# Transposes of 32x32 blocks on VectorE in the block inverse of a delta-rule decoder step

## Chip, cores and metric

The kernel runs on one core of a Trainium2 chip. The metric is the device time of one execution in microseconds; times before are the median of 3 runs. The engines are named as in the profile: PE is TensorE's matmuls, PEld its weight loads, DVE is VectorE, ACT is ScalarE, POOL is GpSimd, SP is the engine whose queue issues most DMAs.

## What is computed

One inference step of a hybrid decoder with two layers, 256 prompt tokens and 8 sequences of 8 sample tokens, all fp32. Each layer projects the tokens once (2048 to some 7000 columns), runs three groups of heads on the columns, projects back, adds, normalizes and runs a SwiGLU block. The change lies in the first group, the gated delta rule (6 heads of 128). Its core, for chunks of C tokens:

```python
gcum = jnp.cumsum(gi, axis=1)
dmat = jnp.exp(jnp.where(tri, gh[..., :, None] - gh[..., None, :], -jnp.inf))
kk = jnp.einsum('bihd,bjhd->bhij', ki, ki)
A = jnp.where(strict, kk * dmat * bh[..., :, None], 0.0)
M = jnp.eye(C, dtype=jnp.float32) + A
...
sol = lax.linalg.triangular_solve(M, jnp.concatenate([vbeta, kbd], -1),
                                  left_side=True, lower=True, unit_diagonal=True)
```

The kernel builds the inverse T of M, a lower triangular matrix with a unit diagonal, from the inverses of its 32x32 diagonal blocks.

## The kernel before

**Dense work.** The 320 tokens are the moving columns of all projections. Every weight is split into a high and a low part in a format that PE multiplies at its fast rate: ScalarE copies the high part (`whi`), VectorE subtracts to get the low part (`wlo`), and each 128x128 weight block gives three matmuls of 128x320, named `xh,whi`, `xl,whi` and `xh,wlo` in the profile. Weights arrive as units of four blocks (128x512, buffer `raw`), twelve matmuls each. There are four buffers of low parts, and the splits run three units ahead of the matmuls.

**Mixers.** The three groups of heads are generators that issue small operations while the dense matmuls of the input and output projection run. Everything is first recorded. A planner (`Program.order`) then puts all operations in an order by its own cost estimates and by the longest tail behind each operation, and only this order is issued; every engine works through its own rows strictly in that order. For PE the planner prefers dense matmuls while small ones of less than the full array collect, and then issues the collected ones together. This document calls one such run of small matmuls between two dense ones a visit. The small matmuls are fp32, and the profile counts each of them as two instructions. Line 671 issues all planned operations, so the profile gives that line to almost everything; the names of the tiles tell operations apart.

**The inverse.** `gdn_prompt` calls `inverse` for two chunks of 128 tokens in each of two half groups of three heads, `gdn_sample` once for each half with 64 tokens; with two layers that makes 8 calls of 128 rows (R) and 4 of 64 rows, each for 3 heads (k). The result `TU` holds T in `tu[:, 0]` and its transpose in `tu[:, 1]`, both as 32x32 blocks side by side: partitions are the rows of the blocks, columns are 3 heads x 32. The algorithm starts with blocks of size 1 and doubles the size. `lt[:, s]` is the part of A (transposed) that level s couples. The start sets T to I - L, for which the transpose of `lt[:, 0]` is made on PE as a matmul with the identity (`cs("idb")`); T's transpose is made by POOL without PE. Each later level (4 with 128 rows, 2 with 64 rows) has two halves on PE: first `lt[:, s]` times T, which ScalarE copies out of PSUM into `p_`; then T times `p_`, and in further matmuls the transpose of that product (`pw[:, 0]` and `pw[:, 1]`). One VectorE subtraction of both parts (192 columns) updates T and its transpose. A half level is one 32x32x32 matmul for each block and head, 12 in the prompt, 6 with the sample tokens.

The users of `TU` multiply with both parts. After both groups of prompt and sample, `gate` multiplies the outputs with the gate and splits them into `oA`, which the output projection reads first.

**Names in the profile.** `g` (in orders `g_0_90`) is the memory of `gdn_prompt`; `c` (`c_0_92`), `blkC` and `gen` hold that of `gdn_sample`; `cst` holds constants, the identity blocks among them; `geng` holds attention and linear-attention data; `bank` is PSUM.

Of the kernel before, what the change touches and what calls it, by code (L numbers as in the profile page):

```python
# [23 lines left out]
D = 2048  # L24
# [96 lines left out]
class Mem:  # L121
    """columns of one SBUF tile handed out and taken back in program order, longest-free or (fit) smallest first"""
# [4 lines left out]
    def alloc_top(self, n):  # L127
        """from the highest end"""
        for a, m, t in sorted(self.free, reverse=True):
            if m >= n:  # L130
                self.free.remove((a, m, t))
                if m > n:
                    self.free.append((a, m - n, t))
                return (a + m - n, n, self.ap[:, a + m - n:a + m])
        return None
# [45 lines left out]
class Clock:  # L181
    """rough engine times, used only to choose the order in which work is issued"""
# [56 lines left out]
class TagTile:  # L239
    """a tile of a tag, made when its turn comes in the final order"""  # L240
# [5 lines left out]
class LazyAP:  # L246
    """access pattern of a TagTile: a stand-in for shapes, and the steps that lead to the real one"""
# [53 lines left out]
def region(ap):  # L301
    """(memory, first and last partition, [(first column, last column)]) of an access pattern"""
    key = None
    if isinstance(ap, LazyAP):
        key, ap = ap.h.key, ap.ap_
    if not isinstance(ap, bass.AP):
        ap = ap[:]
    if "DRAM" in str(ap.space):
        return None
    dims = [tuple(d) for d in ap.ap]  # L310
    w, npart = dims[0]
    p0, c0 = divmod(ap.offset, w)
    run, outer = 1, []
    for s, n in sorted(dims[1:]):
        if n == 1 or s == 0:
            continue
        if s == run or s < run:
            run = (n - 1) * s + run
        else:
            outer.append((s, n))  # L320
    starts = [c0]
    for s, n in reversed(outer):
        starts = [x + s * i for x in starts for i in range(n)]
    if key is not None:
        c = 0
    return (key or ap.name, p0, p0 + npart, [(x, x + run) for x in starts])
# [14 lines left out]
class Program:  # L341
    """operations as they are asked for, put in another order that keeps what they depend on, then issued"""
# [6 lines left out]
    # ---- dependencies  # L349
# [19 lines left out]
    def epoch(self, key):  # L369
        """a bank begins a new use"""  # L370
        if self.seen.get(key):
            self.pre[key] = self.seen[key]
        self.seen[key] = []
        self.mem.pop(key, None)
        for q in range(4):
            self.chain.pop((key, q), None)
# [45 lines left out]
    def _merge(self, g, o, reads, writes, quads):  # L422
        """o runs beside g, in other columns of the array"""
        deps = set()
        for w, aps in ((False, reads), (True, writes)):
            for ap in aps:
                r = region(ap)
                key, p0, p1, spans = r
                if key.startswith("bank"):
                    spans = [(0, 512)]  # L430
                    deps.update(self.pre.get(key, ()))
                    self.seen.setdefault(key, []).append(g.i)
                if w:
                    for q in quads:
                        if (key, q) in self.chain:
                            deps.add(self.chain[(key, q)])
                        self.chain[(key, q)] = g.i
                self._touch(g.i, key, w, p0, p1, spans, deps, g.raw)
        deps.discard(g.i)
        g.preds |= deps  # L440
        g.subs.append((o.fn, o.a, o.kw))
        g.quads = sorted(set(g.quads) | quads)
        i = g.i
        self._cost(o, False, 1)
        g.cost = max(g.cost + 24, o.cost)
        g.busy += 24
        g.load = max(g.load, o.load)
# [62 lines left out]
    # ---- order  # L510
    def order(self):
# [42 lines left out]
        while len(res) < len(ops):  # L554
# [15 lines left out]
            # choose  # L570
# [103 lines left out]
def aps_of(name, a, kw):  # L674
    """(read, written) access patterns of an operation"""
# [43 lines left out]
def emit(nc, pool, psp, T, O, coff, ioff, n_pages):  # L719
# [53 lines left out]
    # ---------------------------------------------------------------- helpers  # L773
# [20 lines left out]
    def rsqrt_small(out, v):  # L794
        """out = v ** -0.5 for a few columns"""
        r0 = 64 if out.shape[0] == 64 else 0
        tt(G, out, v, cs("mhalf", slice(r0, 128)).to_broadcast([128 - r0, out.shape[1]]), ALU.pow)
# [4 lines left out]
    # ---------------------------------------------------------------- tasks  # L802
# [73 lines left out]
    def fb(*bs):  # L876
        for b in bs:
            mix_free.append(b)
# [9 lines left out]
    # ---------------------------------------------------------------- units  # L888
# [5 lines left out]
    def four(W, u, keys, ln):  # L894
        """four output blocks, all of them one k at a time; x is not normalized yet where ln is given"""
# [6 lines left out]
    def one(W, u, key, nk, x, pre=None):  # L902
        """one output block over nk k-blocks, four at a time"""
# [61 lines left out]
    # ---------------------------------------------------------------- weight stream  # L965
# [19 lines left out]
    # ---------------------------------------------------------------- evictions  # L985
# [62 lines left out]
    def small_block(i, key):  # L1048
        """32 outputs: the k-blocks side by side in the four column groups, which stay four partial sums"""
# [15 lines left out]
    # layer norm, first half: t = acc - c for a c near the mean of the token, and its sums. The product that  # L1065
    # follows starts on g t before the sums are known: W (g (t - mu) r + b) = r (W (g t) - mu W g) + W b, with
    # -g and b as two more columns of x
# [79 lines left out]
    def ln_scale(m, e):  # L1147
        """t -> (t - mu) r"""
# [61 lines left out]
    def block_value(key, bi):  # L1210
        """(values, per-row term still to be added or None, memory to free) of a finished block"""
# [72 lines left out]
    # ================================================================ mixers  # L1284
# [60 lines left out]
    # ---------------------------------------------------------------- GDN  # L1345
    # q, k, v are kept as 2 silu(.) = x (1 + tanh(x / 2)); the l2 norm of q and k takes the factor out
# [59 lines left out]
    def gdn_main(l):  # L1406
# [38 lines left out]
        # cumulative decays  # L1445
# [19 lines left out]
        # l2 norms (the blocks hold twice the vectors: 4 eps)  # L1465
# [25 lines left out]
        # output gate  # L1491
# [7 lines left out]
    def gate(l, hi, lo, z, o):  # L1499
        """out = hi/lo of o * z (1 + tanh(z / 2))"""  # L1500
# [18 lines left out]
    def inverse(aq, k, R, get, keep):  # L1519
        """aq: [R, k, 2, N] with A^T at [:, :, 1]; returns handle of TU [R, 2, k, 32] (T | T^T) of the 32-blocks"""  # L1520
# [18 lines left out]
        bb = yield from bank()  # L1539
        pv_ = banks[bb][0:R, 0:32 * k].rearrange("p (h i) -> p h i", h=k)  # L1540
        for h in range(k):
            for b in range(nb):
                sl = slice(32 * b, 32 * b + 32)
                mm(pv_[sl, h], lt[sl, 0, h], cs("idb", sl))
        tt(G, tu[:, 1], idb, lt[:, 0], ALU.subtract)
        tt(V, tu[:, 0], idb, pv_, ALU.subtract)
        fb(bb)
# [3 lines left out]
        for s in range(1, nl):  # L1551
# [10 lines left out]
            pw = banks[bb][0:R, 0:64 * k].rearrange("p (t h i) -> p t h i", t=2, h=k)  # L1562
            for h in range(k):
                for b in range(nb):
                    sl = slice(32 * b, 32 * b + 32)
                    mm(pw[sl, 0, h], tu[sl, 1, h], p_[sl, h])
                for b in range(nb):
                    sl = slice(32 * b, 32 * b + 32)
                    mm(pw[sl, 1, h], p_[sl, h], tu[sl, 1, h])
            tt(V, tu, tu, pw, ALU.subtract)  # L1570
            fb(bb)
            yield
# [3 lines left out]
    def decay_scores(l, g, h0, k, get, keep):  # L1576
        """[R, k, 2, n]: D * s_j * (q k^T | k k^T)^T of token group g, heads h0..h0+k"""
# [31 lines left out]
    def rms_factor(m, out, t1, c=None):  # L1609
        """out = c * rsqrt(c^2 m / 128 + 1e-6) (c = 1 where not given)"""  # L1610
# [10 lines left out]
    def gdn_prompt(l, hs):  # L1621
# [6 lines left out]
        for c in range(2):  # L1628
# [50 lines left out]
            # token-major keys (scaled for the state update) and values  # L1679
# [21 lines left out]
            # right-hand side  # L1701
# [67 lines left out]
    def gdn_sample(l, hs):  # L1769
# [10 lines left out]
        # the upper rows of these columns hold the outputs  # L1780
# [68 lines left out]
    # ---------------------------------------------------------------- differential attention  # L1849
    lam_init = [0.8 - 0.6 * math.exp(-0.3 * l) for l in range(DEPTH)]  # L1850

    def hilo(hi, lo, src, g=None):
        """hi/lo split of src (times the per-partition column g)"""
# [7 lines left out]
    def rope_pair(l, j, t):  # L1861
        """rotate blocks j and j + 1; t holds their rows in the partners' places (zeros where sin is zero)"""
# [12 lines left out]
    def attn_main(l):  # L1875
# [27 lines left out]
        # V of this step, token major  # L1903
# [117 lines left out]
    def attn_scores(l, lsel, getb, get1):  # L2021
# [13 lines left out]
        for pr in range(4):  # L2035
            # q of the two sequences, laid out so that other sequences and maps meet zeros
# [56 lines left out]
    def attn_values(l, vt, getb):  # L2093
# [3 lines left out]
        for quad in range(2):  # L2097
# [35 lines left out]
            # rows of the transpose are (b4, h, q); the output wants (h, b, q)  # L2133
# [9 lines left out]
    # ---------------------------------------------------------------- gated linear attention  # L2143
    def gla_main(l):
# [26 lines left out]
        # running log decay, feature major [128 (2 heads x 64), 3 blocks, tokens]  # L2171
# [28 lines left out]
    def gla_prompt(l, bc, eb, M1):  # L2200
# [10 lines left out]
        # score matrices, transposed: [j, head, i] for both chunks and for the sample tokens  # L2211
# [57 lines left out]
        # k e^{last - bc} (token major) and q e^{bc}  # L2269
# [155 lines left out]
    # ---------------------------------------------------------------- run  # L2425
# [177 lines left out]
```

## Time and profile before

| | us |
|---|---|
| runs: median (lowest, highest) | 3383.41 (3383.02, 3388.16) |
| profiled execution, span from first to last instruction | 3386.1 |
| busy: PE | 3292.8 (97%) |
| busy: DVE | 1976.8 (58%) |
| busy: ACT | 1484.9 (44%) |
| busy: POOL | 596.7 (18%) |
| granted TensorE clock, mean | 0.990 |

The span falls into stretches that repeat with the layer: input projection and mixers (0 to 600 and 1690 to 2270 us), output projection with the end of the mixers and a layer norm (to 780 and 2460 us), and the SwiGLU block (to 1690 and 3386 us). In the SwiGLU blocks PE is busy with dense matmuls alone. In the first two, dense matmuls and visits take turns. A busy share is a mean over these stretches; the cost of one visit is read from the timeline of PE, where rows are in order of start time and equal instructions in a row are merged ("x24").

### The profile page before, as it was taken

The numbers are of one execution on the slowest core, as the hardware profiler recorded it, in microseconds if no ns is written. First come the engines' busy times: TensorE is split into PE (matmuls) and PEld (weight loads), VectorE is DVE, ScalarE is ACT, GpSimd is POOL, SyncE is SP. The second block draws the span as 40 slices with busy tenths as digits, with TensorE's granted clock in tenths as the row PEclk, the third lists the DMA queues.
The fourth block names the chain that finished last, engine by engine and source line by source line (L and its number), as shares of the span: only waits on it lengthen the run. The fifth ranks groups of instructions, "written<-read, shape, count | busy, mean of one in ns | idle before, by whom it ended". The sixth has DMA issues, their size and how long they took to land. (4 is left out here: it accounts for less than half of the span.)

```text
span 3386.1 us, 70352 instructions
## 1 busy us (share of the span) xinstructions
PE 3292.8 (97%) x26570; PEld 3101.2 (92%) x26570; DVE 1976.8 (58%) x3624; ACT 1484.9 (44%) x3059; POOL 596.7 (18%) x825
## 2 busy tenths in 40 slices
PE   9999999999999999999999999999899999999996
PEld 8888787889999999999988887878899999999996
DVE  6666448786445444444876664587954454444446
ACT  5444444445433443344564443453644334433443
POOL 0233423260000000000523333231600000000005
PEclk9999999999999999999999999999999999999998
DMA  6455753434454554544444567434344545454443
GB/s 217 140 175 184 243 189 123 138 118 147 150 150 150 151 150 150 150 150 150 146 145 139 177 213 242 155 116 153 118 147 150 150 150 152 151 150 150 150 150 109
DMA packets 264696, 527.89 MB, mean 156 GB/s; under 512 B 31394, under 2 KB 33570, under 8 KB 264226
## 3 DMA queue, kind: packets, MB, share of 16 engines
q1 hardware_dynamic: 243874, 456.26, 43.8%
q0 software_dynamic: 20480, 67.13, 6.0%
q8 instruction: 208, 3.41, 0.4%
q14 instruction: 134, 1.10, 0.1%
HBM read 506.25 MB, written 16.36 MB: 154 GB/s over the span
## 5 line engine op out<-in xcount | busy, mean ns | idle before, releaser
L671 DVE TENSOR_TENSOR wlo<-raw,whi 128x512 fp32r<-128x512 f32 x1616 | 1166.8, 723 | 1152.9 <-PE bank L671 950.9
L671 ACT CAST whi<-raw 128x512 fp32r<-128x512 f32 x1616 | 999.7, 620 | 1443.2 <-PE bank L671 1351.1
L671 PE MATMUL bank<-xh,whi 128*128 128x320 f32 (+1 forms) x4544 | 1423.0, 313 | 22.3 <-DVE geng L671 10.3
L671 PE MATMUL bank<-xh,wlo 128*128 128x320 f32 (+1 forms) x4544 | 1424.4, 313 | 7.6 <-DVE wlo L671 7.6
L671 PE MATMUL bank<-xl,whi 128*128 128x320 f32 (+1 forms) x4544 | 1420.9, 313 | 0.1
L671 PEld LDWEIGHTS bank<-xh,whi 128*128 128x128 f32 x4544 | 860.4, 189 | 37.9 <-DVE geng L671 11.1
L671 PEld LDWEIGHTS bank<-xh,wlo 128*128 128x128 f32 x4544 | 862.5, 190 | 15.7 <-DVE wlo L671 10.1
L671 PEld LDWEIGHTS bank<-xl,whi 128*128 128x128 f32 x4544 | 860.3, 189 | 15.5 <-issue 11.8
L671 POOL TENSOR_TENSOR geng<-blkB 128x320 f32<-128x320 f32 x8 | 8.1, 1009 | 1747.8 <-DVE blkB L671 1747.8
L671 PE MATMUL bank<-actA,whi 128*128 128x320 f32 x1152 | 254.9, 309 | 0.0
L671 PEld LDWEIGHTS bank<-actA,whi 128*128 128x128 f32 x1152 | 192.7, 188 | 0.0
L671 PE MATMUL bank<-actA,wlo 128*128 128x320 f32 x576 | 177.9, 309 | 0.0
L671 PE MATMUL bank<-actB,whi 128*128 128x320 f32 x768 | 171.2, 310 | 0.0
L671 PE MATMUL bank<-actCh,whi 128*128 128x320 f32 x448 | 138.4, 309 | 0.0
L671 PE MATMUL bank<-actCl,whi 128*128 128x320 f32 x448 | 138.4, 309 | 0.0
L671 PE MATMUL bank<-actCh,wlo 128*128 128x320 f32 x448 | 138.4, 309 | 0.0
L671 PEld LDWEIGHTS bank<-actB,whi 128*128 128x128 f32 x768 | 128.6, 188 | 0.6
L671 PE MATMUL bank<-actB,wlo 128*128 128x320 f32 x384 | 118.9, 310 | 0.1
L671 PE MATMUL bank<-geng,gen 128*32 128x256 f32 (+5 forms) x968 | 109.0, 468 | 5.7 <-DMA geng<-in_ck 4.9
L671 PEld LDWEIGHTS bank<-actA,wlo 128*128 128x128 f32 x576 | 108.3, 188 | 0.0
L671 PEld LDWEIGHTS bank<-g 32*32 32x32 f32 (+2 forms) x2784 | 56.1, 111 | 40.4 <-issue 34.6
L2003 POOL DMA_DIRECT2D geng<-in_cvp x128 | 69.4, 542 | 121.4 <-PE bank L671 100.7
(297 smaller groups left out, 3621.8 us busy)
## 6 DMA issues: line engine op xcount, KB each, us to landing
raw<-in_wgu SPq DMA_DIRECT2D x704, 256.0 KB
raw<-in_win SPq DMA_DIRECT2D x434, 256.0 KB
raw<-in_wd SPq DMA_DIRECT2D x352, 256.0 KB
geng<-in_ck POOLq DMA_DIRECT2D x128, 256.0 KB, 3.9
geng<-in_cvp POOLq DMA_DIRECT2D x128, 256.0 KB, 3.8
raw<-in_wout SPq DMA_DIRECT2D x128, 256.0 KB
c<-in_sgdn SPq DMA_DIRECT2D x6, 512.0 KB
out_gs<-c SPq DMA_DIRECT2D x6, 512.0 KB
```

Source lines behind the costliest of these rows:

```text
L671: fn(*[real(x) for x in a], **{k: real(v) for k, v in kw.items()})
L2003: G.eng.dma_start(out[:, k * 512:k * 512 + 512], src[l, ds(reg, 1)].rearrange(pat))
```

## The change

In `inverse`, the transposed part no longer comes from PE:

- The start makes T's transpose (I minus `lt[:, 0]`) on VectorE rather than on POOL, and T from it with VectorE's transpose of 32x32 blocks. The 12 (or 6) matmuls with the identity, their PSUM bank and the subtraction from it go.
- Each level has only the matmuls for T in its second half; the 12 (or 6) for its transpose go. The subtraction covers 96 columns instead of 192, and a transpose on VectorE then writes the transposed part.

In all, 552 matmuls go (8 x 60 and 4 x 18), and 52 transposes come. All other lines of the diff only take comments away. Its core:

```diff
-        bb = yield from bank()
-        pv_ = banks[bb][0:R, 0:32 * k].rearrange("p (h i) -> p h i", h=k)
-        for h in range(k):
-            for b in range(nb):
-                sl = slice(32 * b, 32 * b + 32)
-                mm(pv_[sl, h], lt[sl, 0, h], cs("idb", sl))
-        tt(G, tu[:, 1], idb, lt[:, 0], ALU.subtract)
-        tt(V, tu[:, 0], idb, pv_, ALU.subtract)
-        fb(bb)
+        tf, tf_ = (ap(TU)[0:R, 32 * k * t:32 * k * t + 32 * k] for t in range(2))
+        tt(V, tu[:, 1], idb, lt[:, 0], ALU.subtract)
+        V.transpose(tf, tf_)
         yield
...
             bb = yield from bank()
-            pw = banks[bb][0:R, 0:64 * k].rearrange("p (t h i) -> p t h i", t=2, h=k)
+            pw = banks[bb][0:R, 0:32 * k].rearrange("p (h i) -> p h i", h=k)
             for h in range(k):
                 for b in range(nb):
                     sl = slice(32 * b, 32 * b + 32)
-                    mm(pw[sl, 0, h], tu[sl, 1, h], p_[sl, h])
-                for b in range(nb):
-                    sl = slice(32 * b, 32 * b + 32)
-                    mm(pw[sl, 1, h], p_[sl, h], tu[sl, 1, h])
-            tt(V, tu, tu, pw, ALU.subtract)
+                    mm(pw[sl, h], tu[sl, 1, h], p_[sl, h])
+            tt(V, tu[:, 0], tu[:, 0], pw, ALU.subtract)
             fb(bb)
+            V.transpose(tf_, tf)
             yield
```

Since the planner sees other operations, it gives a new order to all engines. PE's rows in the first inverse of layer 0, where prompt (`g_0_90`) and sample (`c_0_92`, `blkC`) run side by side, second half of a level, before:

```order
L671 MATMUL bank_84<-c_0_92,blkC 32x32 x2
L671 MATMUL bank_84<-blkC,c_0_92 32x32 x2
L671 MATMUL bank_84<-c_0_92,blkC 32x32 x2
L671 MATMUL bank_84<-blkC,c_0_92 32x32 x2
L671 MATMUL bank_83<-g_0_90 32x32 x24
L671 MATMUL bank_86<-blkC,c_0_92 32x32 x2
L671 MATMUL bank_81<-xh,wlo 128x320
```

and the same place now:

```order
L671 MATMUL bank_81<-xl,whi 128x320
L671 MATMUL bank_84<-blkC,c_0_92 32x32 x6
L671 MATMUL bank_83<-g_0_90 32x32 x12
L671 MATMUL bank_81<-xh,wlo 128x320
L671 MATMUL bank_81<-xh,whi 128x320
```

The sample's half took 12 matmuls, the two directions in alternating pairs (the first four rows before are the last of them), and now takes 6 in one run; the prompt's 24 became 12. Counted over the whole program, PE makes 371 visits in the order before and 363 now.

DVE's rows around the start of the same inverse, before (`blkC` holds the sample's T, `g_0_90` the prompt's):

```order
L671 TENSOR_TENSOR g_0_90<-g_0_90,cst 128x96 x3
L671 TENSOR_TENSOR wlo<-raw,whi 128x512
L671 TENSOR_TENSOR gen<-gen 128x3x3
L671 TENSOR_SCALAR gen<-gen 128x3x3
L671 TENSOR_SCALAR geng<-geng,prm 128x344
L671 SCALAR_TENSOR_TENSOR geng<-geng,prm 128x344
L671 TENSOR_TENSOR wlo<-raw,whi 128x512
L671 TENSOR_TENSOR blkC<-cst,bank_85 64x96
L671 TENSOR_TENSOR g_0_90<-cst,bank_84 128x96
```

and now:

```order
L671 TENSOR_TENSOR blkC<-cst,c_0_92 64x96
L671 TENSOR_TENSOR g_0_90<-g_0_90,cst 128x96
L671 TENSOR_TENSOR c_0_92<-c_0_92,cst 64x96
L671 STREAM_TRANSPOSE blkC<-blkC 64x96
L671 TENSOR_TENSOR g_0_90<-cst,g_0_90 128x96
L671 TENSOR_TENSOR g_0_90<-g_0_90,cst 128x96
L671 STREAM_TRANSPOSE g_0_90<-g_0_90 128x96
L671 TENSOR_TENSOR wlo<-raw,whi 128x512
```

The subtractions from PSUM, which stood behind PE's matmuls with the identity, went; the start now lies between the masks, followed by a transpose each.

PE's rows at the end of layer 0's input projection, before (`cst,geng` are six transposes of attention data, `oA_6354` the first block of the output projection):

```order
L671 MATMUL bank_85<-cst,geng 128x128
L671 MATMUL bank_81<-xl,whi 128x320
L671 MATMUL bank_81<-xh,wlo 128x320
L671 MATMUL bank_79<-oA_6354,whi 128x320 x2
L671 MATMUL bank_79<-oA_6354,wlo 128x320
L671 MATMUL bank_86<-geng 128x128
```

and now, where the same block is `oA_6130`:

```order
L671 MATMUL bank_79<-oA_6130,whi 128x320 x2
L671 MATMUL bank_79<-oA_6130,wlo 128x320
L671 MATMUL bank_79<-oA_6130,whi 128x320 x2
L671 MATMUL bank_86<-cst,geng 128x128
L671 MATMUL bank_84<-cst,geng 128x128
```

The six transposes moved from ahead of the last two matmuls of the input projection to behind the 17th matmul of the output projection.

## Rows read from the trace of the kernel before

**Rows 1.** The page's first part: span, and busy time of each engine

```profile
span 3386.1 us, 70352 instructions
...
PE 3292.8 (97%) x26570; PEld 3101.2 (92%) x26570; DVE 1976.8 (58%) x3624; ACT 1484.9 (44%) x3059; POOL 596.7 (18%) x825
```

**Rows 2.** Waits of PE: who waited for whom, total us, times, longest

```profile
PE bank L671 <- DVE geng L671: 15.1, 6, 3.4
```

**Rows 3.** Timeline of PE, 24 alone: start, us, instruction, count

```profile
345.10 0.31 PE L671 MATMUL bank<-xl,whi 128*128 128x320 f32 x1
345.34 0.39 PE L671 MATMUL bank<-g 32*32 32x32 f32 x24
...
345.91 0.31 PE L671 MATMUL bank<-xh,whi 128*128 128x320 f32 x1
```

**Rows 4.** Timeline of PE, a visit of 48 alone

```profile
277.02 0.31 PE L671 MATMUL bank<-xl,whi 128*128 128x320 f32 x1
277.25 0.62 PE L671 MATMUL bank<-g 32*32 32x32 f32 x48
...
278.05 0.31 PE L671 MATMUL bank<-xh,whi 128*128 128x320 f32 x1
```

**Rows 5.** Timeline of PE, 48 and then 24 beside eight 512-column matmuls

```profile
346.19 0.30 PE L671 MATMUL bank<-xh,wlo 128*128 128x320 f32 x1
346.43 1.06 PE L671 MATMUL bank<-geng,gen 128*32 128x512 f32 x8
347.43 0.62 PE L671 MATMUL bank<-g 32*32 32x32 f32 x48
...
348.23 0.31 PE L671 MATMUL bank<-xl,whi 128*128 128x320 f32 x1
...
352.23 0.31 PE L671 MATMUL bank<-xh,whi 128*128 128x320 f32 x1
...
354.16 0.31 PE L671 MATMUL bank<-xh,wlo 128*128 128x320 f32 x1
```

**Rows 6.** Timeline of PE, the start's visit of 36 (12 sample, 24 prompt)

```profile
113.29 0.31 PE L671 MATMUL bank<-xl,whi 128*128 128x320 f32 x1
...
114.28 0.32 PE L671 MATMUL bank<-xh,whi 128*128 128x320 f32 x1
```

**Rows 7.** Timeline of PE, a visit of 76, both directions of sample and prompt

```profile
121.75 0.31 PE L671 MATMUL bank<-xl,whi 128*128 128x320 f32 x1
121.99 0.25 PE L671 MATMUL bank<-c,blkC 32*32 32x32 f32 x4
...
122.39 0.60 PE L671 MATMUL bank<-g 32*32 32x32 f32 x46
...
123.51 0.31 PE L671 MATMUL bank<-xh,whi 128*128 128x320 f32 x1
```

**Rows 8.** Groups by form: operation, count, busy us, mean ns, idle before

```profile
L671 DVE TENSOR_TENSOR g<-g,bank 128x192 f32<-128x192 f32 x32 | 11.3, 354 | 23.3 <-PE bank L671 23.0
L671 DVE COPY g<-g 32x96 f32<-32x96 f32 x32 | 7.7, 241 | 0.7
L671 DVE TENSOR_TENSOR g<-cst,bank 128x96 f32<-128x96 f32 x8 | 2.0, 250 | 8.5 <-PE bank L671 8.5
...
L671 POOL TENSOR_TENSOR g<-cst,g 128x96 f32<-128x96 f32 x8 | 4.9, 611 | 3.1 <-DVE g L671 2.6 <-DVE gen L671 0.3
```

**Rows 9.** Busy us of each engine in stretches, granted clock, DMA share, GB/s

```profile
0.00:600.00 600.00, 582.01 (x6075) 498.55 (x6077) 376.07 (x861) 278.69 (x706) 178.10 (x312) 0.99 0.56 180
...
560.00:580.00 20.00, 19.65 (x184) 17.09 (x183) 18.54 (x35) 12.66 (x28) 7.19 (x8) 1.00 0.41 133
```

**Rows 10.** Timeline of PE at the end of layer 0's input projection, waits in brackets

```profile
589.31 1.04 PE L671 MATMUL bank<-cst,geng 128*128 128x128 f32 x6 [2.22 <-DVE geng L671]
...
590.68 0.47 PE L671 MATMUL bank<-oA,whi 128*128 128x320 f32 x1
```

**Rows 11.** Instructions on oA, 540 to 600 us: min/median/max ns, first to last start

```profile
L671 DVE TENSOR_TENSOR oA<-blkB,oA x6: 478/479/480, 584.3 to 587.9; 128x320 fp32r<-128x320 f32 x6
```

## The prediction

> **What bounds the kernel now.** Read the page's busy line first [rows 1]: TensorE (PE) is busy for 3292.8 of 3386.1 us. The list of who waited for whom comes next: its longest entry for PE is 15.1 us, behind VectorE (DVE), in the whole span [rows 2]. So PE is the bound, and time goes where PE spends time, not where DVE or ScalarE do. Then read the timeline of PE: the dense projection matmuls start 0.145 us apart, and the small fp32 matmuls of the mixers are put between them in visits. A visit stops the dense stream, so its cost on PE is directly time. I measure it from the start of the last dense matmul before it to the start of the second one after it, less two dense pitches (0.29 us), since the first dense matmul after a visit is late too.
>
> The profile counts every fp32 matmul as two instructions: [rows 3] shows x24 for the 12 matmuls of a half level. By this measure a visit of 24 costs 345.91 - 345.10 - 0.29 = 0.52 us [rows 3], one of 48 costs 278.05 - 277.02 - 0.29 = 0.74 us [rows 4]: about 0.30 us for the visit and 9 ns for each instruction.
>
> **The change part by part.** `inverse` runs 12 times: 8 on prompt chunks (128 rows, one start and four doubling levels, 12 matmuls a half level) and 4 on sample tokens (64 rows, one start and two levels, 6 matmuls a half level).
>
> *Second halves of the prompt.* 32 levels (8 x 4) lose the 12 matmuls that made the transposed part: 24 instructions each, the step from [rows 4] to [rows 3], 0.22 us where the visit stands alone. Most don't stand alone. Beside eight 512-column attention matmuls the visit with 48 takes 348.23 - 346.19 = 2.04 us and the one with 24 takes 354.16 - 352.23 = 1.93 us [rows 5], so there the same 24 are worth 0.11 us. I take the middle, 0.165: 32 x 0.165 = **5.3 us**, bounds 3.5 and 7.0.
>
> *Second halves of the sample.* These lose 6 matmuls in 8 places. In the first inverse of each layer they stand with the prompt's in one visit, where the two directions alternate four instructions at a time on two of the four row groups. That visit of 76 instructions takes 123.51 - 121.75 = 1.76 us [rows 7]. After the change it holds 36 instructions, like the visit of [rows 6], which takes 114.28 - 113.29 = 0.99 us. The step is 0.77 us, of which 0.17 is counted above, so 0.6 more. The order has two such visits in each layer: 4 x 0.6 = **2.4 us**. The four of the second head half lie in long visits, and I give them nothing more (bounds of this term: 1 and 3).
>
> *Starts.* All 12 lose their matmuls with the identity. In each layer one visit holds only these, for prompt and sample together; it goes altogether: 0.99 - 0.29 = 0.70 us [rows 6], twice 1.4 us. The other 8 (6 prompt, 2 sample) shared a visit: 168 instructions at 9 ns make 1.5 us (0.8 at 4.6 ns, the slope of [rows 5]). PE makes 371 visits in the order before and 363 in the order now. Two of the 8 fewer are those that went altogether, which leaves 6 fixed parts of 0.30 us, 1.8 us (0 if repacking alone did it). Together **4.7 us**, bounds 2.2 and 5.
>
> *What DVE takes over.* Each level's subtraction halves, from 354 ns to what 128x96 out of PSUM takes, 250 ns [rows 8]; 52 transposes of 96 columns come (40 prompt, 12 sample). The trace has no DVE transpose. The nearest rows are the 32x96 copy, 241 ns, and the 128x96 subtraction, 250 ns [rows 8]: these move as many elements per partition. I take 0.25 us. Bounds are 0.24, and 0.72 if each of the three 32-column blocks took what such a copy takes. The start's second subtraction moves from POOL, 611 ns [rows 8], to DVE. Net DVE work: 52 x 0.25 - 40 x 0.1 = +9 us in all (33 at the upper bound). The cover is DVE's idle time: 376 of 600 us busy in the first mixer stretch [rows 9]. Without cover a transpose would delay the low halves of the weights (`wlo`), which PE needs; these run three units ahead, some 5 us. Time on the path: **0**.
>
> The Trainium skill (VectorE: DVE Perf Modes, The three transpose paths) gives 311 ns for a 128x128 bf16 transpose on VectorE. An estimate at that price would be 52 x 0.311 - 4 = 12 us of DVE work and the same sum. No run shown so far has the fp32 form.
>
> *The chain inside an inverse.* The first half of a level reads only the untransposed part, so the transpose lies beside that half and not before it. The start loses a whole PE visit, and visits of one inverse are 8.46 / 2 = 4.2 us apart (from [rows 6] to [rows 7] are two). The delta rule's chain therefore ends earlier by about that much for each inverse.
>
> *The wait at the end of the input projection.* Six transposes (`cst,geng`) stand two dense matmuls ahead of the output projection, and PE waits 2.22 us for them [rows 10]. In the new order they come 17 dense matmuls (2.5 us) later, behind the first output block. That wait can go, but other waits will come with a new order, since operations were put elsewhere nearly everywhere. I take **2 us** of gain for the 4.4 in both layers, with -5 to +5 for all waits.
>
> *Sum:* 5.3 + 2.4 + 4.7 + 2 = 14.4 us from 3386.1 gives 3371.7. The profiled span is 2.7 us above the median of the runs, 3383.41; so **3369.0 us**. Bounds of the PE terms (6.7 and 15) and of the waits together give 3360 to 3382.
>
> **The rivals.**
> *The chain to the gate ends the stretch, not PE.* The first output block needs the gated delta-rule output `oA`. Its last DVE operation starts at 587.9 [rows 11], PE reads it from 590.68 [rows 10], and DVE is busy 18.54 of 20 us just before [rows 9]. If this chain didn't move, PE could come only 590.68 - 588.4 = 2.3 us earlier in each layer: 3383.4 - 4.6 = 3379 us. Against it: the chain contains the inverses that get shorter, and the output order leaves `oA` at the same place in the stream of weight splits.
>
> *Every removed matmul costs PE a slot of its own.* By the visit of [rows 7], 0.77 us for 40 instructions, an instruction is worth 19 ns and not 9. If that held everywhere (narrow blocks following one another on the same row group, not beside each other), 1104 instructions would give 21 us, and 3362 us. For it: that visit. Against it: the 9 ns between [rows 3] and [rows 4], where four row groups take turns. The Trainium skill (TensorEngine Tiling, Instruction Overhead) puts about 60 cycles on each matmul, 25 ns, by which 27.6 us would go (an estimate); the trace's 9 ns doesn't bear it out for these.
>
> *The transposes hold up VectorE: slower.* In the first inverse of a layer a level takes 8.46 us, and DVE has about 37% of it free [rows 9], 3.2 us, plus 0.2 from the narrower subtractions. Two transposes (prompt and sample) fit as long as one takes under 1.7 us. Beyond that the splits queued behind them in DVE's order come late and PE starves. At 3 us each it costs 2 x 3 - 3.4 = 2.6 us in each of five steps and two layers, 26 us: 3395 us. Against it: the copies and subtractions of the same size at 0.24 to 0.25 us [rows 8].
>
> That the change might not do what it says is no rival: the order shows 552 fewer matmuls and 52 transposes on DVE.
>
> **How the numbers follow.** Forecast (3369, own range 3362 to 3376) 0.62; gate chain (3379) 0.18; a slot for each matmul (3362, 3358 to 3364) 0.14; slower 0.06. What a measurement of this kernel can tell from no change is about 0.2%, 6.8 us: faster is under 3376.6. The forecast lies there but for 0.03, the third case wholly, the gate chain not: faster 0.73, within 0.2% 0.21, slower 0.06. The range 3360 to 3383 takes in the forecast, the gate chain and most of the third case.
>
> **What the profile after would show.** PE has 1104 fewer instructions; second-half visits of the prompt have 24 instructions; transposes take about 0.25 us in the groups by line; PE's busy time falls by 10 to 14 us while its waits stay near the old sum. PE waiting on `oA` at the end of the input projection speaks for the gate chain. Alone-standing visits of 24 at 0.52 us as before, with the total down by 20, would speak for something I haven't priced. Transposes above 1.7 us would make the prediction wrong on the other side.

## The result and the profile after

| | median us | runs |
|---|---|---|
| before | 3383.22 | 4, 3381.1 to 3388.16 |
| after | 3349.14 | 4, 3347.22 to 3350.11 |

The ratio is 0.9897, 95% interval 0.9883 to 0.9911: 34.1 us faster, where 14.4 was forecast, and below the range's end of 3360. The first lines of the page of after answer [rows 1]:

```profile
span 3346.9 us, 68139 instructions
...
PE 3262.9 (97%) x25466; PEld 3079.6 (92%) x25466; DVE 1978.1 (59%) x3676; ACT 1480.5 (44%) x3059; POOL 595.8 (18%) x813
```

PE has 1104 instructions fewer, as said, but its busy time falls by 29.9 us and not by 10 to 14. DVE's new rows weigh 8.9 us more than the old ones, as worked out (9); other DVE operations add up to 7.6 us less, so its busy time stays where it was. The list of PE's waits in after (who waited for whom: total us, times, longest) adds up to 57.9 us, before to 66.8; against [rows 2]:

```profile
PE bank L671 <- DVE geng L671: 13.0, 7, 3.4
```

The groups by form of after (count, busy us, mean ns) answer [rows 8]: the transpose takes 270 ns, the narrower subtraction 248.

```profile
L671 DVE STREAM_TRANSPOSE g<-g 128x96 f32<-128x96 f32 x40 | 10.8, 270 | 0.8
...
L671 DVE TENSOR_TENSOR g<-g,bank 128x96 f32<-128x96 f32 x32 | 8.0, 248 | 9.7 <-PE bank L671 9.7
```

The timeline of PE in after has a visit of 24 alone, for [rows 3], and the end of layer 0's input projection, for [rows 10]:

```profile
337.70 0.30 PE L671 MATMUL bank<-xh,whi 128*128 128x320 f32 x1
337.94 0.39 PE L671 MATMUL bank<-g 32*32 32x32 f32 x24
338.26 0.41 PE L671 MATMUL bank<-xl,whi 128*128 128x320 f32 x1
338.51 0.31 PE L671 MATMUL bank<-xh,wlo 128*128 128x320 f32 x1
...
566.08 0.55 PE L671 MATMUL bank<-cst,blkC 128*128 128x128 f32 x3 [0.46 <-ACT geng L671]
...
568.09 0.46 PE L671 MATMUL bank<-oA,whi 128*128 128x320 f32 x2
```

338.51 - 337.70 - 0.29 = 0.52 us: the visit costs what it did. The price of a smaller visit was not the prediction's, as the timeline of PE shows, first in before with 18 alone, then in after with 12 alone:

```profile
160.41 0.30 PE L671 MATMUL bank<-xh,wlo 128*128 128x320 f32 x1
160.65 0.38 PE L671 MATMUL bank<-g 32*32 32x32 f32 x18
...
161.21 0.31 PE L671 MATMUL bank<-xl,whi 128*128 128x320 f32 x1
```

```profile
148.97 0.31 PE L671 MATMUL bank<-xl,whi 128*128 128x320 f32 x1
149.21 0.38 PE L671 MATMUL bank<-g 32*32 32x32 f32 x12
...
149.77 0.31 PE L671 MATMUL bank<-xh,whi 128*128 128x320 f32 x1
```

Both cost 0.51 us. So 12, 18 and 24 instructions cost nearly the same, 0.51 to 0.52 us, and only from there to 48 (0.74) does the size count; 0.30 us and 9 ns for each instruction would make 0.41 us of a visit of 12.

The wait of 2.22 us is gone, 0.46 stands there, and PE reads `oA` 22.6 us earlier (568.09 for 590.68). By the number of the dense matmul, the 3500th (in layer 0's SwiGLU) starts at 743.3 instead of 765.1, the 13000th (layer 1's) at 2366.0 instead of 2403.4. Between the mixers nothing changes. The costs of all visits, by the prediction's measure, add up to 469.8 us before and 434.1 after (all runs of other matmuls between two matmuls with weights, 370 and 362 of them in the traces), which is 35.7 of the span's 39.2. So the gain lies in the visits, at nearly three times the 12.4 us worked out for them; these costs include the waits and the slower stretches that fall into visits. The span differs by more than the medians because the profiled execution of before was the longest of its four.

### The profile page after: what moved, and what is told of

Read it like the earlier page. It is cut to its first block, busy times and chain, and to the rows that moved or that the text cites. A ratio compares the mean times of both kernels' runs of the same rounds, so it can differ in the third digit from the quotient of the medians.

```text
span 3346.9 us, 68139 instructions
## 1 busy us (share of the span) xinstructions
PE 3262.9 (97%) x25466; PEld 3079.6 (92%) x25466; DVE 1978.1 (59%) x3676; ACT 1480.5 (44%) x3059; POOL 595.8 (18%) x813
## 5 line engine op out<-in xcount | busy, mean ns | idle before, releaser
L671 PE MATMUL bank<-xh,whi 128*128 128x320 f32 (+1 forms) x4544 | 1420.8, 313 | 22.1 <-DVE geng L671 10.2
L671 PEld LDWEIGHTS bank<-xl,whi 128*128 128x128 f32 x4544 | 858.8, 189 | 10.8 <-issue 7.1
L1995 POOL DMA_DIRECT2D geng<-in_ck x128 | 70.4, 550 | 124.2 <-PE bank L671 88.6
```

What stands on the lines that cost most here:

```text
L671: fn(*[real(x) for x in a], **{k: real(v) for k, v in kw.items()})
L1995: G.eng.dma_start(out[:, k * 512:k * 512 + 512], src[l, ds(reg, 1)].rearrange(pat))
```

## The experiments

Three theories: **T1**, a new order. The planner put nearly everything elsewhere, and some 20 us are waits that only the old order has. **T2**, the removed work itself: the shorter chain of the inverse ends these waits in any order. **T3**, each removed matmul held PE for some 30 ns. The first pair of kernels swaps work and order. Matmuls are counted here and in the expectations as the profile counts them, two instructions for each (1104 for the 552 removed).

**New work, old order.** The planner sees the old operations; the removed ones are not issued.

```
+                prog.ghost = True      # planned, not issued
                 for b in range(nb):
                     sl = slice(32 * b, 32 * b + 32)
                     mm(pw[sl, 1, h], p_[sl, h], tu[sl, 1, h])
-            tt(V, tu, tu, pw, ALU.subtract)
+                prog.ghost = False
...
+            planned(tu, tu, pw, [], update)   # 96-column subtract, then the transpose
```

> The work of the kernel after, issued in the order of the kernel before: the planner still sees the 1104 small matmuls, and they are left out when the program is written; the 96-column subtraction and the transpose stand where the 192-column subtraction stood. Three theories of why the kernel after gained 34 us and not 14. T1, the new order: the removed work is worth the 12 to 14 us that visits of small matmuls cost by their length, and the other 20 us come from waits of TensorE that stood in the old order (for DMAs of caches, for VectorE behind a queue) and do not stand in the new one. Then this kernel keeps these waits and takes 3367 to 3373 us. T2, the removed work itself: the shorter chain inside each inverse ends the waits in any order. Then it takes 3347 to 3356 us, and the 2.2 us wait before the last subtraction of the input projection goes. T3, each removed matmul holds its own place of some 30 ns: TensorE's busy time falls by 30 us as it did, and the time is 3350 to 3355 us in any order.

**3371.0 us** (ratio 0.997, 0.996 to 0.998), 11.0 under before on the same chip. T2 and T3 fall for this order. Its waits of PE show part of why (the longest ones in the stretch 100 to 260 us; first before, then this kernel, then after, which has only these two):

```profile
PE bank L671 <- DMA c<-in_sgdn: 2.1, 1, 2.1
PE bank L671 <- DVE g L671: 1.8, 1, 1.8
PE bank L671 <- DMA geng<-in_ck: 1.4, 1, 1.4
...
```

```profile
PE bank L671 <- DMA geng<-in_ck: 2.6, 1, 2.6
PE bank L671 <- DVE g L671: 2.0, 2, 1.8
PE bank L671 <- DVE blkC L1587: 0.7, 2, 0.5
PE bank L671 <- DMA c<-in_sgdn: 0.6, 1, 0.6
...
```

```profile
PE bank L671 <- DVE sq L671: 0.8, 1, 0.8
PE bank L671 <- DVE sk L671: 0.8, 1, 0.8
```

The old order keeps these waits with the lighter work. The one for `c` shrinks and the one for `in_ck` grows; the new order has none of the three here. Over the whole span PE's waits add up to 67.8 us in this kernel, 66.8 before and 57.9 after. So waits by themselves are 9 to 10 us of the 20 that T1 gives them, not all. The wait of [rows 10] stays as well, as the timeline of PE in this kernel shows:

```profile
580.29 0.88 PE L671 MATMUL bank<-cst,geng 128*128 128x128 f32 x6 [2.23 <-DVE geng L671]
```

One such wait on SyncE's queue (timeline; start, us, transfer): before sends the state's load `c` at 133.76 and PE comes for it at 137.2, waiting until 139.29; after sends it at 126.82 and PE reads at 130.44 without a wait:

```profile
133.76 0.37 SPq L671 DMA_DIRECT2D c<-in_sgdn  x1
```

```profile
126.82 0.33 SPq L671 DMA_DIRECT2D c<-in_sgdn  x1
```

The load isn't sent later against PE: PE comes 3.4 us after the sending in before and 3.6 us after it in after. What differs is the load itself. Its last packet (the 4096-byte packets of the trace) ends 5.0 us after the sending in before and 3.1 us after it in after. Why it took longer there wasn't tried.

A wait costs more than itself. Timeline of PE in the kernel with new work and old order, and under it busy times in three stretches (us, PE, PEld, DVE, ACT, POOL, then the granted clock):

```profile
179.46 0.55 PE L671 MATMUL bank<-cst,g 128*128 128x128 f32 x3 [1.81 <-DVE g L671]
...
180.42 0.47 PE L671 MATMUL bank<-xh,wlo 128*128 128x320 f32 x1
180.68 0.47 PE L671 MATMUL bank<-xh,whi 128*128 128x320 f32 x1
...
185.04 0.31 PE L671 MATMUL bank<-xl,whi 128*128 128x320 f32 x1
185.19 0.32 PE L671 MATMUL bank<-xh,wlo 128*128 128x320 f32 x1
```

```profile
174.00:177.00 3.00, 3.00 (x24) 2.60 (x23) 2.35 (x7) 1.23 (x3) 2.45 (x3) 1.00 0.44 122
180.00:182.00 2.00, 2.00 (x10) 2.00 (x9) 0.79 (x4) 1.11 (x2) 0.00 (x0) 0.53 0.41 99
185.00:187.00 2.00, 2.00 (x18) 2.00 (x17) 1.06 (x3) 0.40 (x2) 0.19 (x1) 1.00 0.10 38
```

After the wait of 1.81 us the mean granted clock is 0.53, nearly all of it at the lower of the two levels (1.2 and 2.4 GHz), and dense matmuls start 0.26 us apart instead of 0.15. The seven steps from 180.15 to 182.02 take 1.87 us instead of 1.02, and the 0.85 us more counts as busy time. In the profiles 69.0 us of before stand at the lower level, 58.6 of this kernel and 45.8 of after (some 23 of each at the very end). This is part of why PE's busy time fell by 30 us although the removed matmuls are worth a third of that.

**Old levels, new order.** The 864 matmuls of the levels and the 192-column subtraction are back; the order is that of after.

```
+                        nc.tensor.matmul(out, lhsT, rhs, **kw)      # planned
...
+                            for c in range(nb):                     # not planned
...
+                                nc.tensor.matmul(pt[q, h], real(p_[q, h]), real(tu[q, 1, h]), **kw)
```

> The order of the kernel after, with 864 of the 1104 removed matmuls back: at each level the transposed half is again made by matmuls, right behind the first half, and the 192-column subtraction stands in place of the 96-column one and its transpose. The starts stay as in the kernel after. T1 (the new order gives 20 of the 34 us): the second halves cost what their length costs, 5 to 10 us, and the waits stay away: 3354 to 3360 us. T2 (the removed work ends the waits): the waits come back with the work, 3370 to 3378 us. T3 (30 ns for each matmul): 864 x 30 ns = 26 us more, 3375 us.

**3354.4 us**, 5.2 above after: 6 ns for each matmul. T2 and T3 fall. The Trainium skill (TensorEngine Tiling (Array Packing), Instruction Overhead) puts about 60 cycles on each matmul; 25 ns on each of the 864 would make it 21.6 us, an estimate. The measurement decides against that sum for these 32x32 blocks, which the code spreads over the row groups.

**Other orders, same work.** One constant of the planner, `PW` (3000 to 2900 or 3100) or `PB` (1000 to 1050):

```
-        sticky, PB, PW = False, 1000.0, 3000.0
+        sticky, PB, PW = False, 1000.0, 2900.0
```

> The kernel before with another order and no other change: the planner's patience with a late operation is 2900 ns in place of 3000, which orders the work anew in most places. It shows how much a new order is worth by itself. T1: a new order alone moves this kernel by up to 10 to 20 us in either direction, so 3365 to 3400 us, with other waits than before. T2 and T3: the old work sets the waits whatever the order, 3378 to 3388 us.

> The kernel after with another order and no other change (patience 2900 ns in place of 3000). T1: the kernel after had a good draw of orders; another draw is 5 to 20 us slower, 3352 to 3370 us. T2 and T3: the removed work is worth 34 us in any order, 3344 to 3354 us.

> The kernel before in a third order (patience 3100 ns), no other change. The first other order took 3369.8 us, 12 us less than the kernel before. If the order's worth is a draw, this one lies between 3362 and 3388 us; if the kernel before had a rarely bad order, near 3370 us again.

> The kernel after in a third order (patience 3100 ns), no other change. The second took 3353.4 us, the first 3349. If the removed work is worth 12 us beside the draw of the order, this one lies 8 to 20 us below the kernel before in its orders: 3348 to 3362 us. If the change also ends waits in any order: 3345 to 3353 us.

> The kernel before in a fourth order: the planner collects 1050 ns of small work in place of 1000 before it sends a visit; no other change. The three orders so far took 3382, 3370 and 3374 us. A further draw of the same kind: 3364 to 3385 us. Below 3360 us it would show that the old work too has orders as good as those of the kernel after.

> The kernel after in a fourth order (1050 ns of small work for a visit), no other change. The three so far took 3349, 3353 and 3347 us. A further draw of the same kind: 3344 to 3358 us. Above 3360 us it would show that the three were lucky.

The old work took **3369.8, 3373.5** and **3387.6 us**, the new **3353.4, 3347.4** and **3359.1**. A constant changed by 3 to 5% moves the old work by -12 to +6 us against before on the same chip, a spread as wide as the whole edit was forecast to be worth. 3369.8 speaks for T1 alone; 3353.4 lies in both ranges of its expectation and decides nothing; 3347.4 lies just under the range for a work worth 12 us, in the one for waits that end in any order. Both orders at 1050 end above what was expected even of a further draw: the spread had still been taken too narrow. The best, 3347.4 (3343.2 to 3351.5), can't be told from after.

**The start alone, in the old order** (levels as before):

```
+        prog.ghost = True
         ...
                 mm(pv_[sl, h], lt[sl, 0, h], cs("idb", sl))
+        prog.ghost = False
...
+        planned(tu[:, 0], idb, pv_, [tu[:, 1]], lambda **kw: nc.vector.transpose(real(tf), real(tf_)))
```

> The kernel before, in its own order, with one part of the change alone: the start of each inverse takes the transposed form from one transpose on VectorE, and its 240 small matmuls against the identity are left out; the levels stay as before. The prediction priced the starts at 4.7 us (2.2 to 5). By that and with the old order's waits in place, 3377 to 3381 us. If the removed matmuls cost 30 ns each instead, 7 us less than before: 3375 us. If the start's shorter chain ends waits further on, 3370 us or less.

**3374.6 us** against 3382.4: 7.8 us, where 4.7 was forecast with a bound of 5. The 95% interval of the ratio (0.9972 to 0.9991) makes it 3.0 to 9.5 us, so 4.7 is not excluded. T3's figure for this run (3375) is right and the prediction's range (3377 to 3381) is missed; T3 fails in the two runs above. PE's waits keep nearly the old sum (66.5 us), so the start didn't end them.

**Each transpose twice**, in the order of after:

```
+            nc.vector.transpose(real(out), real(in_))
+            nc.vector.transpose(real(out), real(in_))
```

> The kernel after in its own order, with each of the 52 transposes issued twice on VectorE (the second writes the same values again): 14 us more work on VectorE, 0.27 us more in each step of the inverses' chain. It prices what the change puts on VectorE. If VectorE's part is off the path, as the prediction took it, 0 to 1 us slower: 3349 to 3351 us. If each transpose of the chain reaches the path in full, 52 x 0.27 us = 14 us: 3363 us. If they hold up the weights' low halves behind them, some part of that with more waits of TensorE for VectorE's wlo.

**3350.4 us**, 1.3 above after and hardly outside its runs (up to 3350.1), with 13.1 us more DVE work (page: 1991.2 for 1978.1). PE's wait for `wlo` is 11.7 us, after has 12.0. What the change puts on DVE lies beside PE.

**New work in two more old orders:**

> The work of the kernel after in the order of the kernel before with patience 2900 (3369.8 us with the old work): again the 1104 small matmuls are planned and left out. In the first order that step took 3382 to 3371 us, 11 us. If the removed work is worth 11 us by itself in any order: 3357 to 3361 us. If more of it was hidden behind the first order's waits, which this order does not have: 3352 to 3357 us. If the removed work were worth nothing without its waits: 3365 us or more.

> The work of the kernel after in the order of the kernel before with patience 3100 (3373.5 us with the old work). 11 us for the removed work in any order: 3360 to 3365 us. More where the order's waits don't cover it: 3353 to 3360 us.

**3359.0** and **3367.0 us**, 10.8 and 6.5 less than the old work in the same orders; the second gains less than was expected. With the first order's 11.0, the new work is worth 9.4 us on average where the order stays; the runs of one kernel spread over 5 to 10 us, so the three are not told apart.

**Each part planned for itself.** The levels' hunk or the start's hunk of the change alone, nothing planned that isn't issued.

> The change at the levels alone (transposed halves by VectorE's transposes, the starts as before), planned for itself. If the levels let the planner find the better orders: 3350 to 3362 us. If the start does: the work alone, 5 us below the old work's orders, 3366 to 3380 us. If it is a draw: anywhere between.

> The same in another order (patience 3100 ns). If the levels let the planner find the better orders: 3350 to 3362 us. If the start does: 3366 to 3380 us.

> The change at the start alone (no matmuls against the identity, no bank, one transpose; the levels as before), planned for itself. In the old order this part was worth 7.7 us. If the start lets the planner find the better orders: 3352 to 3362 us. If the levels do: 5 to 8 us below the old work's orders, 3363 to 3380 us.

> The same in another order (patience 3100 ns). If the start lets the planner find the better orders: 3352 to 3362 us. If the levels do: 3363 to 3380 us.

**3381.8** and **3385.3 us** for the levels: 864 matmuls less and nothing gained. **3376.5** and **3372.3** for the start. Neither part brings the good orders: the start lies in the range that stood for "the levels do", and the levels lie above both of theirs. What the levels' orders have stands at the end of layer 0's input projection (first levels kernel; timeline of PE, then the granted clock of two stretches, in the third column from the end):

```profile
578.50 0.47 PE L671 MATMUL bank<-cst,geng 128*128 128x128 f32 x1 [1.75 <-DVE geng L671]
...
582.10 0.64 PE L671 MATMUL bank<-oA,whi 128*128 128x320 f32 x1 [0.91 <-DVE oA L671]
582.54 0.47 PE L671 MATMUL bank<-oA,wlo 128*128 128x320 f32 x1
...
584.53 0.63 PE L671 MATMUL bank<-oA,whi 128*128 128x320 f32 x1 [1.26 <-DVE oA L671]
584.96 0.47 PE L671 MATMUL bank<-oA,wlo 128*128 128x320 f32 x1
```

```profile
562.00:567.00 5.00, 4.78 (x56) 4.12 (x54) 4.91 (x10) 2.22 (x7) 1.86 (x2) 1.00 0.28 67
...
579.00:584.00 5.00, 3.27 (x11) 2.05 (x9) 5.00 (x5) 2.48 (x6) 4.87 (x8) 0.50 0.00 0
```

The dense matmuls run out, PE follows the gated output block by block, and the clock halves. That is the first rival's place, and it is slow: the profiles of the two levels kernels have 90.5 and 92.7 us at the lower clock, before 69.0, of which about half is lost where PE is busy. That is some 11 us, more than the levels' work is worth where the order is held (2.8 to 8.9 us). Waits of PE for `oA` stand in six kernels of the series: 4.3 and 6.4 us (levels), 6.0 and 5.1 (start), 5.5 (old work, 1050) and 3.0 (new work, 1050). The last two are the slowest orders of their work; before and after have none.

**Old levels in two more new orders:**

> The order of the kernel after with patience 2900 (3353.4 us with the new work), with the 864 matmuls and the wide subtraction of the old levels back in it. If the order planned for the new work is good in itself: 5 us more, 3356 to 3361 us. If it is good only with the lighter work: the waits come back, 3368 us or more.

> The same in the order of the kernel after with patience 3100 (3347.4 us with the new work). Good in itself: 3350 to 3355 us. Good only with the lighter work: 3362 us or more.

**3362.4** and **3350.2 us**, 8.9 and 2.8 above the new work. The first falls between its two ranges, the second into the first. With 3354.4 all three stay below every order planned for the old work with that work in it. But they hold the new start, which that work lacks: with its 7.8 us added (an estimate), the first is level with the best old order, 3369.8, and the other two lie some 8 to 12 us below it. The plainer comparison is the same new work in both kinds of order (second and fourth row below): the orders planned for it are 21.9, 5.6 and 19.6 us faster. So these orders are good mostly in themselves.

All together (us; columns are `PW` 3000, 2900 and 3100, and `PB` 1050 with `PW` 3000):

| order planned for | work issued | 3000 | 2900 | 3100 | 1050 |
|---|---|---|---|---|---|
| old | old | 3383.2 | 3369.8 | 3373.5 | 3387.6 |
| old | new | 3371.0 | 3359.0 | 3367.0 | |
| new | old levels, new start | 3354.4 | 3362.4 | 3350.2 | |
| new | new | 3349.1 | 3353.4 | 3347.4 | 3359.1 |
| old start, new levels | the same | 3381.8 | | 3385.3 | |
| new start, old levels | the same | 3376.5 | | 3372.3 | |

What an order is worth can be read in the six profiles with the new work, old order less new order (us):

| | 3000 | 2900 | 3100 |
|---|---|---|---|
| span | 21.8 | 5.1 | 23.3 |
| PE's waits | 9.9 | 0.2 | 6.9 |
| time at the lower clock | 12.8 | -2.6 | 22.1 |

Where PE is busy about half the time at the lower clock is lost (1.87 us for 1.02 above), so waits and clock together make some 16, -1 and 18 us. They follow the span from pair to pair and fall short of it by 5 to 6 us each time, which stays unexplained.

## Why the prediction was wrong

Faster, and by more than can be missed, was right; the size was not. The low end of the range did not follow from its own bounds either: 15 us of PE terms and 5 of waits give 3363, not 3360. Step by step:

- **The removed matmuls** (second halves and starts, 12.4 us): about right as a sum. With the order held, 11.0, 10.8 and 6.5 us were measured. Within it the starts look too cheap (7.8 for 4.7, not beyond the noise). The levels look too dear: 3374.6 - 3371.0 = 3.6 us in the old order, and 5.2, 8.9 and 2.8 in the new, for 7.7. Two readings behind these terms were wrong. A visit of 12, 18 or 24 alone costs 0.51 to 0.52 us, and not 0.30 and 9 ns for each instruction. And the last four instructions in the visit of [rows 7] start 0.28 us behind the others and belong to the next half level; they were counted among the 40 that go, and 36 go.
- **What DVE takes over** at nothing: right. 270 ns for a transpose, against 250 taken, and doubling them moved the time by 1.3 us, which the runs hardly tell from nothing.
- **The chain inside an inverse** one visit shorter: the traces agree. The visit at 113.2 us is the start before and the first level after. What follows from that wasn't priced.
- **The waits** (2 us, -5 to +5): this is the step that failed. It named one wait, which did go, and gave the rest of a wholly new order 5 us either way. It also priced a wait by its length alone, though [rows 10] shows more: the matmul on `oA` behind the wait of 2.22 us takes 0.47 us, where dense ones take 0.31, since the clock was at its lower level there. In this pair the order was worth 34.1 - 11.0 = 23 us. Of these, some 8 are the draw, that is luck: before lies 4.7 above the mean of its four orders (3378.5), after 3.1 below its own (3352.3). The other 15 belong to what all four orders planned for both parts share (the means lie 26.2 apart, of which 9.4 are the work, and 17 the planning; with four orders a side that scatter over 18 and 12 us, the 17 is known to some 5 us). The range needed the spread of orders, and the prediction had no row for it: one trace of one order can't show it.
- **The rivals.** *Gate chain:* not in this pair, since `oA` moved with the rest; it is what other orders run into. *A slot for each matmul:* 3362 would have been nearer, but by accident: 5.2 us for 864 is 6 ns and not 19. *Transposes hold up VectorE:* no, by the doubling.

**Left open:** why the planner leaves fewer waits, and less time at the lower clock, in orders planned for both parts (some 17 us on average), while it doesn't for one part. The planner counts small work before it sends a visit and follows the longest tail, and both parts change both. Which of these it is wasn't tried.

## What to carry to other kernels

Where a planner sets the order, an edit has two prices: its work with the order held, and the new order. Measure the first by planning the old operations and leaving them out, and the second by drawing a few orders of both kernels; a single pair mixes them. A part that gains nothing alone, as the levels here, may still be worth keeping with another: judge the whole over several orders.

## What was not expected of the hardware

A wait of 1.8 us on PE was followed by a granted clock of 0.53 and dense matmuls 0.26 us apart, so one late input was paid twice. Small fp32 matmuls on 32x32 blocks cost only 3 to 10 ns for each instruction in a visit that happens anyway (2.8 to 8.9 us for 864), and a visit alone costs 0.51 us with 12 of them and 0.52 us with 24.
